# A gate's early load behind a numbered piece, and rings of four places in the first half of an output projection

## The chip, the cores and the metric

The kernel runs on one core of a Trainium2 chip. The metric is device time in microseconds from the runs' own clock. A core has TensorE (PE in the profile, its weight loads PEld), VectorE (DVE), ScalarE (ACT), GpSimd (POOL) and SyncE (SP). SyncE does no arithmetic here: it issues nearly all transfers, in order, and waits where one of them must wait.

## The reference

One layer: a norm, a modulation from the conditioning vector c, a gated short convolution between two projections, a gated residual and a last norm. All in float32, for 256 tokens, width D = 2048, inner width E = 4096.

```python
h = rmsnorm(x, norm_g)
mod = silu(c) @ ada_w + ada_b
shift, scale, gate = split(mod, 3)
h = h * (1 + scale) + shift
b_gate, c_gate, v, g = split(h @ w_in, 4)          # w_in: 2048 x 16384
u = causal_depthwise_conv(c_gate * v, conv_w)      # 3 taps
y = (b_gate * u * silu(g)) @ w_out                 # w_out: 4096 x 2048
return rmsnorm(x + gate * y, final_g)
```

## The kernel before

Each factor of a product is split in a high and a low part, rounded to TensorE's one-pass float32 form: `hi` by a cast on ScalarE (L380), `lo` by a subtraction on VectorE (L385). A product is three matmuls: high by high, low by high, high by low. The tokens h lie transposed in SBUF in both parts (`hT`, 16 groups k of 128 rows); the weights come in *pieces* of 1 MB, loaded by SyncE into rings of buffers, split, and multiplied.

The stages, with the names that the profile's lines bear:

- Start: x, its norm, the first sums of the modulation.
- `mm_s` (L545): half of the columns of w_in, while the modulation's shift and scale are still being summed.
- `mm_b` (L545), the *two-tile stage*: the other half, in 64 pieces (8 pairs of column tiles x 4 quarters x 2 halves of k). A piece is one load (L804), one high and one low part, and 48 products (2 tiles x 8 k x 3).
- The output projection, first for columns 0 to 1023 (`mm_w`, banks `mm_1`, `mm_7`), then for 1024 to 2047 (`mm_o`), L888. A piece covers two k of w_out by 1024 columns. A *plain* piece takes 24 matmuls. The pieces 8 to 15 (in the second half 10 to 15) use seven block products in place of eight (`seven`, 21 matmuls): they need sums of the weights' blocks (`sums_o`, three operations on VectorE, L769 to L773) and `forms` of the tokens' blocks.
- The end: residual, last norm, stores.

Beside the two-tile stage two more jobs run. The gate: 32 loads of ada_w (`at_g`), multiplied and summed on VectorE (`gacc`, L709, L711), then folded over the partitions by GpSimd in seven rounds of transfer and addition (L715 to L717) and added to the row `gate_row` in DRAM (L719), once for each 512 columns. And `early_weights`, which after each of certain pieces does a unit of later work: the sums of a sevens piece for columns 1024 to 2047, or one of two pieces already multiplied by the gate (`gated`); both are stored to DRAM (`made`) and loaded in the output stage. The dictionary `EARLY` says after which piece (counted from 0) which unit comes. One unit is the gate's early load (L786): 512 columns of `gate_row`, broadcast over the partitions into `turned`, a part of the scratch tile z, for the gated pieces.

What sets the order: within `short_conv_layer` a scheduler places each engine's instructions by priority, a timeline that it models, and the dependences it is given; `tc.add_manual_dep` adds one that only fixes an order. A queue is then served in that order: an instruction that waits holds up all behind it on its engine. L786 had no tie of that kind.

Places: the pool `wpool` has three buffers each of the kinds raw, hi and lo. In the output stage pieces and sums go to the lo buffers and low parts to the raw buffers. The large tile `big` takes the room of `hT` once the tokens are read; it holds x, the weights of the last norm (`fg`) and a scratch tile, and before that three more places for pieces and sums in the first 1024 columns (`wide_ring`, a ring of six) and one in the second (`next_ring`).

Of the kernel before, what the change touches and what calls it, by code (L numbers as in the profile page):

```python
# [117 lines left out]
def short_conv_layer(ctx: ExitStack, tc: tile.TileContext, x, c, norm_g, ada_w, ada_b, w_in, conv_w, w_out, final_g, out):  # L118
# [19 lines left out]
        return slots.tile(shape, dtype, tag="slot", name=name)  # L138

    nth = {"raw": 0, "hi": 0, "lo": 0}  # L140

    def pad(n, name, pool=wpool):
        pool.tile([P, n], F32, tag=name, name=name, bufs=1)

    def w_tile(kind, name, dtype=F32, i=None):

        if i is None:
            i = nth[kind] % 3
            nth[kind] += 1
        return wpool.tile([P, SLOT], dtype, tag=f"{kind}{i}", name=name, bufs=1)  # L150

    pad(32, "line4")
# [146 lines left out]
    junk = hpool.tile([P, TT, HX], F32, tag="big", name="junk")  # L299
    for t in range(TT):  # L300
        for dh in range(2):
            if t == 0:
# [12 lines left out]

    KB = KT - 2
    hT = hpool.tile([P, KB, 2 * T], F32R, tag="big", name="hT")
    hT2 = hpool.tile([P, KT - KB, 2 * T], F32R, tag="big2", name="hT2")  # L320

    def tokens(k, part):
        return (hT[:, k] if k < KB else hT2[:, k - KB])[:, part * T : (part + 1) * T]

    hh_ = [tokens(k, 0) for k in range(KT)]
    hl_ = [tokens(k, 1) for k in range(KT)]
# [347 lines left out]
    nc.gpsimd.dma_start(gate_row, ada_b[0:1, 2 * D : 3 * D])  # L674

    def gate_columns(c0, n):
        flat = gate_slots[c0 // 1024].rearrange("p h s f -> p (h s f)").bitcast(F32)
# [5 lines left out]
    def load_gate(j):  # L683

        c0 = j * 1024
        nc.sync.dma_start(gate_columns(c0, 1024), gate_row[0:1, c0 : c0 + 1024].partition_broadcast(P))

    gate_todo = [(dc, j) for dc in range(4) for j in range(0, KT, 2)]
    gacc = [None]
# [75 lines left out]
    passed = [0]  # L765

    def sums_of(b, s):

# [6 lines left out]
    def early_weights():  # L775

        while to_store:
            unit, sums = to_store.pop()
            made[unit] = dram.tile([P, SLOT], F32, tag=f"made{len(made)}", name="made")
            nc.scalar.dma_start(made[unit], sums)  # L780
        unit = EARLY.get(passed[0])
        passed[0] += 1
        if unit is None:
            return
        if unit == "gate":
            nc.sync.dma_start(turned, gate_row[0:1, 3 * W : 4 * W].partition_broadcast(P))  # L786
            return
        raw, sums = raw_tile("raw_u"), w_tile("lo", "sums_u")
        blocks, out = (v.rearrange("p (b f) -> p b f", f=W) for v in (raw, sums))
        if not isinstance(unit, int):  # L790
            load_o(raw, unit[1] * EP, EP, 3 * W, W)
            nc.vector.tensor_tensor(out=out, in0=blocks, in1=turned.unsqueeze(1).to_broadcast([P, EP, W]), op=ALU.mult)
        else:
            load_o(raw, 2 * unit, 2, 2 * W, 2 * W)
            list(sums_of(blocks, out))
        to_store.append((unit, sums))

    for ct in range(NS, NCT, 2):
        for q in QUARTERS:
            bank = psum.tile([P, CT, T], F32, tag="mm", name="mm_b")[:, 0:2]  # L800
            col = q * E + ct * P
            for kp in range(0, KT, KP):
                raw = raw_tile("raw")
                nc.sync.dma_start(  # L804
                    raw.rearrange("p (k f) -> p k f", k=KP),
                    w_in[0, kp * P : (kp + KP) * P, col : col + 2 * P].rearrange("(k p) f -> p k f", p=P),
                )
                hi, lo = split(raw, SLOT)
                for m in range(2):
                    for i in range(KP):  # L810
                        k = kp + i
                        o = slice((i * 2 + m) * P, (i * 2 + m + 1) * P)
                        for j in range(3):
                            product(bank[:, m, :], hi[:, o], lo[:, o], k, j, k == 0 and j == 0, m == 0, k == KT - 1 and j == 2)
                gate_piece()
                early_weights()
            z = zs[q // 2][:, q % 2]
            if q == 1:
                nc.scalar.copy(z, bank)
                zc = z  # L820
            elif q == 2:
                nc.vector.tensor_tensor(out=zc, in0=bank, in1=zc, op=ALU.mult)
                for j in range(2):
                    conv(ct + j, z[:, j, :], zc[:, j, :])
                u = z
            elif q == 3:
                ended_silu[0] = nc.scalar.activation(z, bank, AF.Silu)
                nc.vector.tensor_tensor(out=u, in0=u, in1=z, op=ALU.mult)
            else:
                nc.vector.tensor_tensor(out=u, in0=bank, in1=u, op=ALU.mult)  # L830
                split_y(ys[ct // 2], u)
                if ct // 2 in SEVEN:
                    token_forms(ct // 2, u)
# [2 lines left out]
        gate_piece()  # L836


    big = hpool.tile([P, 3 * D + W], F32, tag="big", name="big")
    xh = big[:, 0 : TT * D].rearrange("p (h t f) -> p h t f", h=2, t=TT)  # L840
    HD = D // 2

    def xr(t, c0, n):
        return xh[:, c0 // HD, t, c0 % HD : c0 % HD + n]

    def load_x(h):
        for t in range(TT):
            nc.sync.dma_start(xh[:, h, t], x[t * P : (t + 1) * P, h * HD : (h + 1) * HD])

    fg = big[:, TT * D : 3 * D]  # L850
    u2 = big[:, 3 * D :]
    ends = [z.rearrange("p a b f -> p (a b f)").rearrange("p (h f) -> p h f", h=2) for z in zs]

    places6 = [None] * 3 + [big[:, i * SLOT : (i + 1) * SLOT] for i in range(3)]
    taken, ending = [0], [False]

    def wide_ring(name):

        i = taken[0] % 6 if not ending[0] else 0
        taken[0] += 1  # L860
        return w_tile("lo", name) if places6[i] is None else places6[i]
# [35 lines left out]
    def weighted(t, c0, n, pr, at):  # L897


        r = xr(t, c0, n)  # L900
        nc.scalar.activation(pr, r, AF.Square, scale=D**-0.5, accum_out=fsq[:, t, at : at + 1])
        nc.vector.tensor_tensor(out=r, in0=r, in1=fg[:, c0 : c0 + n], op=ALU.mult)

    def seven(j, raw, sums, ready, bank, p1, p6, p75, opens, last):

# [34 lines left out]
        add(ends[0][:, 0], p75[:, 1], u2)  # L940
        add(ends[1][:, 0], p75[:, 1], ends[1][:, 1])

    def columns(c0, order, sevens, bank, p1, p6, p75, whole, loads=None, ring=None):


        for n, j in enumerate(order):
            raw = w_tile("raw", "raw_o") if n == 0 and c0 == 0 else ring("raw_o")
# [8 lines left out]
            if loads:  # L956
                loads(n)
            if j in sevens:
                sums = ring("sums_o")
                if ready:  # L960
                    nc.sync.dma_start(sums, made[j])
                seven(j, raw, sums, ready, bank, p1, p6, p75, j == sevens[0], j == sevens[-1])
                if j == sevens[-1]:
                    gather(p1, p6, p75)
                continue
            hi, lo = split(raw, SLOT, "raw")
# [13 lines left out]
    def wide_bank(name):  # L980
# [3 lines left out]
    wide = [wide_bank("mm_w") for _ in range(TT)]  # L984
    columns(
        0, (0, 1, 8, 2, 9, 3, 10, 4, 11, 5, 12, 13, 6, 14, 15, 7), SEVEN,
        lambda t, d: wide[t][:, d], *extra_banks(), p75, True, load_ends, wide_ring,
    )
    for t in range(TT):
        c = ends[t].rearrange("p h f -> p (h f)")  # L990
# [7 lines left out]
    def finish(t):  # L998
# [4 lines left out]
        for c0, n, vector in ((0, 512, True), (512, 512, False), (1536, 512, True), (1024, 512, False)):  # L1003
            dd = slice(c0, c0 + n)
            r = xr(t, c0, n)
            if c0 == 1536:
                nc.vector.scalar_tensor_tensor(out=r, in0=po[t], scalar=fs, in1=fg[:, dd], op0=ALU.mult, op1=ALU.mult)
# [7 lines left out]
    taken[0] = 0  # L1015

    def next_ring(name):

        i = taken[0] % 4
        taken[0] += 1  # L1020
        return big[:, SLOT : 2 * SLOT] if i == 3 and taken[0] <= 12 else w_tile("lo", name)

    halves = [wide_bank("mm_o") for _ in range(2)]
    p75 = wide_bank("mm_7")
    po = extra_banks()
    columns(
        2 * W, (0, 1, 10, 2, 11, 3, 12, 13, 8, 14, 15, 9), SEVEN_2,
        lambda t, d: halves[d][:, t], *po, p75, False, lambda n: load_x(1) if n == AT_X else None, next_ring,
    )

    def out_mm(bank, t, ep, hi, lo):
# [78 lines left out]
```

## Time and profile before

| | |
|---|---|
| runs | 919.80, 920.08, 920.12 us; median 920.08 |
| the profiled execution | 917.02 us, span 915.2 us |
| mean granted TensorE clock | 0.991 |
| read from HBM, written | 237.86 MB, 10.50 MB |
| DMA over the span | 281 GB/s mean |
| TensorE on the chain that ended last | 79% (mm_s 38%, mm_b 27%) |

The profile is of one execution, and that one was 3 us shorter than the median; durations are read from it, differences are then set against the median. A busy share of an engine is over the whole span. The chain of work is followed back from the last instruction: what released each step, or the instruction before it on its engine. In rows of single instructions the bracket holds the idle time ahead of it and what ended it.

### The profile page before, as it was taken

To read this page: it belongs to the slowest core of one execution; us is meant where nothing else is said; L and a number is where in the kernel's file an instruction comes from. 1 tells how busy PE (TensorE), PEld (TensorE's weight loads), DVE (VectorE), ACT (ScalarE), POOL (GpSimd) and SP (SyncE) were. 2 spreads that over 40 slices of the span, in tenths; PEclk is the share of its full clock that TensorE was granted. 3 is DMA by queue.
4 is the path that set the end of the run, shared out by engine and by line. 5 is a ranking of instruction groups with operands and counts; after the bars stand their busy time and mean duration, and the time that the engine had idled before them with its cause. 6 is when DMAs were issued, how large, how long until landed. Compare 5 with 4: busy or idle time off the path is not lost.

```text
span 915.2 us, 16520 instructions
## 1 busy us (share of the span) xinstructions
PE 888.6 (97%) x6977; PEld 849.9 (93%) x6977; DVE 695.4 (76%) x693; ACT 490.5 (54%) x436; POOL 88.0 (10%) x108
## 2 busy tenths in 40 slices
PE   7999999999999999999999999949999999999996
PEld 4999999999999999999999999949999988778885
DVE  5889998889987876858865786537667668999775
ACT  6768866565558765644344434234434454545553
POOL 0000000010000234410132012400000000000000
PEclk9999999999999999999999999979999999999999
DMA  9999999999997688777877889489889877686872
GB/s 307 368 370 365 365 321 354 341 363 351 380 344 258 189 279 238 237 215 222 271 230 219 273 270 307 142 286 301 290 286 289 306 264 244 197 294 235 302 280 92
DMA packets 164873, 257.29 MB, mean 281 GB/s; under 512 B 7668, under 2 KB 106580, under 8 KB 162624
## 3 DMA queue, kind: packets, MB, share of 16 engines
q1 hardware_dynamic: 159680, 239.89, 79.5%
q0 software_dynamic: 3840, 7.94, 3.2%
q10 hardware_dynamic: 1280, 8.43, 2.3%
q8 instruction: 54, 0.88, 0.4%
q14 instruction: 19, 0.16, 0.0%
HBM read 237.86 MB, written 10.50 MB: 271 GB/s over the span
## 4 chain that ended last, share of the span: by engine, by line
PE 79%; DMA 11%; DVE 4%; ACT 2%; POOL 2%; issue 1%; SPq 0%; ACTq 0%; POOLq 0%; DVEq 0%
PE mm_s L545 38%; PE mm_b L545 27%; PE mm_o L888 6%; PE mm L888 4%; DMA z<-gacc 3%; PE mm_w L888 3%; DMA at_g<-in_ada_w_dram 3%; DVE lo L385 2%; DMA at<-in_ada_w_dram 2%; ACT hi L380 2%; POOL gacc L717 1%; DMA raw_o<-in_sc_w_out_dram 1%; DMA raw<-in_sc_w_in_dram 1%; POOL z L715 0%; DVE gacc L711 0%
## 5 line engine op out<-in xcount | busy, mean ns | idle before, releaser
L545 PE MATMUL mm_b<-hT,hi 128*128 128x256 f32 x2048 | 349.9, 277 | 11.4 <-ACT hi L380 11.4
L545 PE MATMUL mm_s<-hT,hi 128*128 128x256 f32 x2048 | 336.3, 277 | 0.0
L545 PEld LDWEIGHTS mm_b<-hT,hi 128*128 128x128 f32 x2048 | 309.3, 188 | 11.6 <-ACT hi L380 11.6
L545 PEld LDWEIGHTS mm_s<-hT,hi 128*128 128x128 f32 x2048 | 299.7, 188 | 0.2
L545 PE MATMUL mm_b<-hT,lo 128*128 128x256 f32 x1024 | 283.4, 277 | 1.5 <-DVE lo L385 1.5
L545 PE MATMUL mm_s<-hT,lo 128*128 128x256 f32 x1024 | 261.7, 277 | 0.0
L380 ACT CAST hi<-raw 128x2048 fp32r<-128x2048 f32 (+1 forms) x66 | 123.8, 1876 | 206.9 <-PE mm_b L545 94.0
L385 DVE TENSOR_TENSOR lo<-raw,hi 128x2048 fp32r<-128x2048 f32 (+1 forms) x66 | 153.3, 2328 | 78.6 <-ACT hi L380 63.1
L545 PEld LDWEIGHTS mm_b<-hT,lo 128*128 128x128 f32 x1024 | 192.9, 188 | 1.8 <-DVE lo L385 1.8
L545 PEld LDWEIGHTS mm_s<-hT,lo 128*128 128x128 f32 x1024 | 182.7, 188 | 0.0
L385 DVE TENSOR_TENSOR lo<-raw_s,hi 128x2048 fp32r<-128x2048 f32 (+1 forms) x80 | 149.0, 1868 | 29.9 <-ACT hi L380 29.3
L380 ACT CAST hi<-raw_s 128x2048 fp32r<-128x2048 f32 (+2 forms) x81 | 124.0, 1541 | 70.2 <-PE mm_s L545 42.9
L515 DVE SCALAR_TENSOR_TENSOR gv<-at,silu_c,gv 128x512 f32<-128x512 f32 x105 | 78.8, 751 | 10.3 <-DMA at<-in_ada_w_dram 8.6
L568 ACT COPY acc<-mm_s 128x1024 f32<-128x1024 f32 x54 | 54.6, 1011 | 26.9 <-PE mm_s L545 26.8
L717 POOL TENSOR_TENSOR gacc<-gacc,z 128x512 f32<-128x512 f32 x28 | 44.2, 1577 | 103.4 <-DMA z<-gacc 103.4
L888 PE MATMUL mm_w<-hi,y 128*128 128x512 f32 x160 | 51.4, 390 | 0.3 <-ACT hi L380 0.3
L711 DVE SCALAR_TENSOR_TENSOR gacc<-at_g,silu_c,gacc 128x512 f32<-128x512 f32 x60 | 45.0, 749 | 7.4 <-DMA at_g<-in_ada_w_dram 6.3
L888 PE MATMUL mm_o<-hi,y 128*128 128x512 f32 x152 | 48.3, 389 | 0.0
L582 ACT COPY mm_s<-acc 128x1024 f32<-128x1024 f32 x38 | 38.6, 1015 | 2.6 <-DVE acc L571 1.8
L380 ACT CAST hi<-raw_o 128x2048 fp32r<-128x2048 f32 x14 | 26.7, 1909 | 22.1 <-DMA raw_o<-in_sc_w_out_dram 16.8
L385 DVE TENSOR_TENSOR lo<-raw_o,hi 128x2048 fp32r<-128x2048 f32 x14 | 32.1, 2289 | 6.8 <-ACT hi L380 6.7
L888 PEld LDWEIGHTS mm_w<-hi,y 128*128 128x128 f32 x160 | 30.0, 188 | 6.9 <-ACT hi L380 0.7
(191 smaller groups left out, 745.6 us busy)
## 6 DMA issues: line engine op xcount, KB each, us to landing
raw<-in_sc_w_in_dram SPq DMA_DIRECT2D x64, 1024.0 KB, 6.2
raw_s<-in_sc_w_in_dram SPq DMA_DIRECT2D x47, 1024.0 KB, 8.2
at<-in_ada_w_dram SPq DMA_DIRECT2D x126, 256.0 KB, 7.9
raw_o<-in_sc_w_out_dram SPq DMA_DIRECT2D x17, 1024.0 KB, 6.0
raw_s<-in_sc_w_in_dram SPq DMA_DIRECT2D x33, 512.0 KB, 7.2
at_g<-in_ada_w_dram SPq DMA_DIRECT2D x32, 512.0 KB, 8.2
raw_u<-in_sc_w_out_dram SPq DMA_DIRECT2D x8, 1024.0 KB, 5.7
made<-sums_u ACTq DMA_DIRECT2D x8, 1024.0 KB, 6.9
```

The lines of the kernel that those rows point to most:

```text
L380: nc.scalar.copy(hi[:, :n], raw[:, :n])
L385: last_low[0] = nc.vector.tensor_tensor(out=lo[:, :n], in0=raw[:, :n], in1=hi[:, :n].bitcast(F32), op=ALU.subtract)
L515: nc.vector.scalar_tensor_tensor(out=gv, in0=at4[:, i], scalar=c_k, in1=gv, op0=ALU.mult, op1=ALU.add)
L545: mm = last_mm[0] = nc.tensor.matmul(dst, w, h[k], start=begins and left, stop=ends, skip_group_check=True)
L568: nc.scalar.copy(acc[ch, q], bank)
L582: nc.scalar.copy(bank, acc[ch, q])
L711: nc.vector.scalar_tensor_tensor(out=ga, in0=at3[:, i, :], scalar=s, in1=ga, op0=ALU.mult, op1=ALU.add)
L717: nc.gpsimd.tensor_tensor(out=ga, in0=ga, in1=turned, op=ALU.add)
L888: nc.tensor.matmul(dst, y[a], b, start=opens and i == 0, stop=ends and i == 2, skip_group_check=True)
```

## The change

Two parts, and moves that come with them.

The gate's early load gets a dependence on the load of the 56th piece of the two-tile stage, so it stands behind it on SyncE. The sums move from pieces 35, 39, ... 55 to 32, 36, ... 52, the gate's load from 58 to 55, the gated pieces from 59 and 62 to 56 and 60.

`hT` becomes five tiles (`b0`, `b1`, `b2` of four k each, `b3` and `big2` of two), each given back when its own readers are done; `junk` and later x (`xr`), the last norm's weights and gate (`closing`) and the scratch `u2` take their places one by one. In the first 1024 output columns b0, b1 and b2 serve as a fourth buffer for pieces and sums (lo), for high parts (hi) and for low parts (raw), until the eleventh piece (n = 10); from the fourteenth (n = 13) b1 is the fourth lo buffer, until the sixth piece of the second half. The rings of six and four are gone. The gate's columns 0 to 1023 are loaded into the second half of `closing`, 1024 to 2047 into the place of piece 8's forms; the last norm's weights are loaded in two halves. `opens` and `last` of the sevens pieces now go by the order of the pieces.

```diff
     nth = {"raw": 0, "hi": 0, "lo": 0}
+    fourth = {}
...
         if i is None:
-            i = nth[kind] % 3
-            nth[kind] += 1
+            size = 4 if kind in fourth else 3
+            i = nth[kind] % size
+            nth[kind] = i + 1
+        if i == 3:
+            return hpool.tile([P, SLOT + 64], dtype, tag=fourth[kind], name=name)[:, 16 : 16 + SLOT]
         return wpool.tile([P, SLOT], dtype, tag=f"{kind}{i}", name=name, bufs=1)
...
-    hT = hpool.tile([P, KB, 2 * T], F32R, tag="big", name="hT")
-    hT2 = hpool.tile([P, KT - KB, 2 * T], F32R, tag="big2", name="hT2")
+    hT = [hpool.tile([P, SLOT + 64], F32R, tag=f"b{g}", name="hT") for g in range(3)]
+    hT += [hpool.tile([P, 4 * T], F32R, tag=tag, name="hT") for tag in ("b3", "big2")]
...
-    EARLY = {35 + 4 * i: j for i, j in enumerate(SEVEN_2)}
-    EARLY.update({58: "gate", 59: ("gated", LAST[0]), 62: ("gated", LAST[1])})
+    EARLY = {32 + 4 * i: j for i, j in enumerate(range(10, 16))}
+    EARLY.update({55: "gate", 56: ("gated", LAST[0]), 60: ("gated", LAST[1])})
...
         if unit == "gate":
-            nc.sync.dma_start(turned, gate_row[0:1, 3 * W : 4 * W].partition_broadcast(P))
+            load = nc.sync.dma_start(turned, gate_row[0:1, 3 * W : 4 * W].partition_broadcast(P))
+            tc.add_manual_dep(load.ins, last_load[0].ins.name, after, reason="the gate is done by then")
             return
...
     def load_ends(n):
 
-        ending[0] = n >= AT_END
-        if n == AT_END - 2:
-            load_gate(0)
+        if n == AT_END - 3:
+            fourth.clear()
         elif n == AT_END:
             load_x(0)
-        elif n == AT_END + 1:
-            nc.sync.dma_start(fg, final_g.rearrange("(o d) -> o d", o=1).partition_broadcast(P))
-            load_gate(1)
-
+            closing.append(hpool.tile([P, D], F32, tag="b2", name="closing"))
+            load_fg(0)
+            load_broadcast(HD, gate_row[0:1, 0:HD])
+            fourth["lo"] = "b1"
+
+    fourth.update({"lo": "b0", "hi": "b1", "raw": "b2"})
...
+    def load_last(n):
+
+        if n == AT_X - 3:
+            fourth.clear()
+        elif n == AT_X:
+            load_x(1)
+            nc.sync.dma_start(gate_columns(HD, HD), gate_row[0:1, HD:D].partition_broadcast(P))
+            load_fg(1)
```

How it moves SyncE's queue in the second half of the two-tile stage (raw: pieces, raw_u: the early units' weights, z: the gate's early load). Before:

```order
L804 DMA raw<-in_sc_w_in_dram 128x8x256 x4
L755 DMA raw_u<-in_sc_w_out_dram 128x2x1024
L804 DMA raw<-in_sc_w_in_dram 128x8x256 x4
L755 DMA raw_u<-in_sc_w_out_dram 128x2x1024
L786 DMA z_4482<-gate_row 128x512
L804 DMA raw<-in_sc_w_in_dram 128x8x256 x4
```

The same queue after, from the fifth early unit:

```order
L757 DMA raw_u<-in_sc_w_out_dram 128x2x1024
L808 DMA raw<-in_sc_w_in_dram 128x8x256 x4
L757 DMA raw_u<-in_sc_w_out_dram 128x2x1024
L808 DMA raw<-in_sc_w_in_dram 128x8x256 x3
L789 DMA z_4485<-gate_row 128x512
L808 DMA raw<-in_sc_w_in_dram 128x8x256
L757 DMA raw_u<-in_sc_w_out_dram 128x4x512
```

The gate's load stood behind the 40th piece and the second early unit; it now stands behind the 56th and the sixth.

TensorE where the two-tile stage ends and the output begins (mm_w and mm_1 are banks; hi_8428 and lo_8430 are the parts of piece 0, hi_8458 of piece 1, hi_8489 of piece 8, the third in turn). Before:

```order
L545 MATMUL mm_b_8291<-hT2_174,lo_8354 128x256
L888 MATMUL mm_w_8422<-hi_8428,y0_3413 128x512
L888 MATMUL mm_w_8422<-lo_8430,y0_3413 128x512
L888 MATMUL mm_w_8422<-hi_8428,y0_3413 128x512 x2
L888 MATMUL mm_w_8422<-lo_8430,y0_3413 128x512
```

After (hi_8431 and lo_8433 are the parts of piece 0, hi_8492 of piece 8):

```order
L550 MATMUL mm_b_8300<-hT_177,lo_8359 128x256
L891 MATMUL mm_w_8425<-hi_8431,y0_3416 128x512
L891 MATMUL mm_w_8426<-hi_8431,y0_3416 128x512
L891 MATMUL mm_1_8427<-hi_8492,y8_4475 128x512
L891 MATMUL mm_w_8425<-lo_8433,y0_3416 128x512
```

The first matmul of piece 8 stood behind all of piece 0 and two matmuls of piece 1; it now stands third, ahead of the first use of piece 0's low part.

SyncE in the output's first half. Before, from the sixth piece on (big: places of the ring of six, x and the last norm's weights; gate: the gate's halves):

```order
L755 DMA raw_o<-in_sc_w_out_dram 128x2x1024 x2
L686 DMA gate_4480<-gate_row 128x1024
L755 DMA big<-in_sc_w_out_dram 128x2x1024 x2
L686 DMA gate_4481<-gate_row 128x1024
L755 DMA raw_o<-in_sc_w_out_dram 128x2x1024 x2
L755 DMA big<-in_sc_w_out_dram 128x2x1024 x2
L755 DMA raw_o<-in_sc_w_out_dram 128x2x1024 x2
L848 DMA big<-in_x_dram 128x1024 x2
L961 DMA big<-made 128x2048
L871 DMA big<-in_final_g_dram 128x2048
```

After, from the stage's start:

```order
L757 DMA raw_o<-in_sc_w_out_dram 128x2x1024 x7
L1024 DMA gate_4483<-gate_row 128x1024
L757 DMA raw_o<-in_sc_w_out_dram 128x2x1024 x5
L852 DMA xr<-in_x_dram 128x1024 x2
L858 DMA closing<-in_final_g_dram 128x1024
L858 DMA closing<-gate_row 128x1024
L757 DMA raw_o<-in_sc_w_out_dram 128x2x1024 x6
```

One of the two loads of the gate behind which pieces stood is gone from there; x, half of the last norm's weights and half of the gate stand in front of the 13th piece, where x and the weights stood behind the 15th.

More of the change, by code (lines that the diff above doesn't have):

```diff
@@ L298, in short_conv_layer @@
     rstd = const.tile([P, TT], F32, tag="rstd", name="rstd")
-    junk = hpool.tile([P, TT, HX], F32, tag="big", name="junk")
+    junk = hpool.tile([P, TT, HX], F32, tag="b0", name="junk")
     for t in range(TT):
@@ L941, in gather, with columns @@
         add(ends[1][:, 0], p75[:, 1], ends[1][:, 1])
-    def columns(c0, order, sevens, bank, p1, p6, p75, whole, loads=None, ring=None):
+    def columns(c0, order, sevens, bank, p1, p6, p75, whole, loads=None):
+        in_turn = [j for j in order if j in sevens]
         for n, j in enumerate(order):
-            raw = w_tile("raw", "raw_o") if n == 0 and c0 == 0 else ring("raw_o")
+            raw = w_tile("raw" if n == 0 and c0 == 0 else "lo", "raw_o")
             ready = c0 > 0 and j in made
@@ L958, in columns @@
             if j in sevens:
-                sums = ring("sums_o")
+                sums = w_tile("lo", "sums_o")
                 if ready:
                     nc.sync.dma_start(sums, made[j])
-                seven(j, raw, sums, ready, bank, p1, p6, p75, j == sevens[0], j == sevens[-1])
-                if j == sevens[-1]:
+                seven(j, raw, sums, ready, bank, p1, p6, p75, j == in_turn[0], j == in_turn[-1])
+                if j == in_turn[-1]:
                     gather(p1, p6, p75)
```

50 lines of the change are left out of this document (22 added, 28 removed).

## The prediction

> **What bounds the kernel now.** I read the page first: busy shares, then the slices (two of its 40-slice lines, TensorE's busy tenths and granted clock).
>
> ```profile
> PE 888.6 (97%) x6977; PEld 849.9 (93%) x6977; DVE 695.4 (76%) x693; ACT 490.5 (54%) x436; POOL 88.0 (10%) x108
> PE   7999999999999999999999999949999999999996
> PEclk9999999999999999999999999979999999999999
> ```
>
> TensorE is the bound, at 97% of 915.2 us. It has one hole in mid-kernel: in the 27th slice (595 to 618 us) it is busy four tenths, and its clock falls. The waits of TensorE (waited for: total us, times, longest) say how much all its holes are worth:
>
> ```profile
> PE mm_b L545 <- ACT hi L380: 11.4, 1, 11.4
> PE mm_b L545 <- DVE lo L385: 1.5, 1, 1.5
> PE mm L888 <- DVE lo L918: 1.0, 2, 0.6
> PE mm_w L888 <- ACT hi L380: 0.3, 1, 0.3
> ```
>
> The first two are the hole; the last two, 1.3 us, are all else that an edit after the start can win. The chain of work that ended last names the cause (start, length, what):
>
> ```profile
> 377.06 125.02 PE mm_b L545 x1103
> ...
> 542.97 0.55 POOL z L715
> ...
> 593.92 2.13 DMA gate_row<-gacc
> 596.25 0.34 SPq L786
> 596.70 7.37 DMA raw<-in_sc_w_in_dram
> 604.15 1.91 ACT hi L380
> 606.08 2.30 DVE lo L385
> 608.42 126.55 PE mm_b L545 x1102
> ```
>
> The gate row's last transfer ends at 596.05. SyncE's L786 (the gate's early load) goes 0.2 us later, the next piece behind it, and that piece's landing, high part and low part precede TensorE's restart. SyncE's own waits confirm it: it stood at L786 for 15.9 and 3.8 us.
>
> ```profile
> SPq L786 <- DMA z<-gacc: 15.9, 1, 15.9
> SPq L786 <- DMA gate_row<-gacc: 3.8, 1, 3.8
> ```
>
> **The change part by part.**
>
> *The gate's load behind the 56th piece.* A piece is 48 products. At 125.02 / 1103 = 0.1133 us each it takes 5.44 us, and the stage's 64 pieces take 3072 x 125.02 / 1103 = 348.2 us. Begun at 377.06 without a hole the stage ends at 725.3. It really ended where the first product of the output starts:
>
> ```profile
> 740.23 0.39 PE L888 MATMUL mm_w<-hi,y 128*128 128x512 f32 x1
> ```
>
> So the hole costs 740.2 - 725.3 = 15.0 us. That is the idle 12.9 of the first two waits plus about 2 of slow clock, which the stretches show (length, busy and count, granted clock, DMA share, GB/s):
>
> ```profile
> 598.00:605.00 7.00, 0.00 (x0) 0.50 0.99 309
> 610.00:612.00 2.00, 2.00 (x14) 0.69 0.91 284
> 612.00:614.00 2.00, 2.00 (x20) 1.00 0.97 262
> ```
>
> After the change the load stands behind piece 56 (counted from 1). Loads run ahead: the 33rd piece was issued at 533.46 (row below) and multiplied from 377.06 + 32 x 5.44 = 551.1, 17.7 us later. The 57th would be issued near 377.06 + 56 x 5.44 - 17.7 = 664, 68 us after the row was done. Its reader, the first gated piece, moves with it. What was queued behind it on SyncE no longer waits. Saved: 15.0.
>
> *The early sums three pieces sooner.* Six sums and two gated pieces keep their count and durations; each moves three or two pieces forward. The delicate one is the first: it enters where VectorE still works off the gate's sums. SyncE's issues, VectorE's low parts, and the two landings (issue, size, us) that begin at 544.9 and at 547.5:
>
> ```profile
> 533.46 14.01 SPq L804 DMA_DIRECT2D raw<-in_sc_w_in_dram  x4
> 542.58 4.49 DVE L385 TENSOR_TENSOR lo<-raw,hi 128x2048 fp32r<-128x2048 f32 x2
> 544.90 2.57 SPq L804 DMA_DIRECT2D raw<-in_sc_w_in_dram  x2
> raw<-in_sc_w_in_dram SPq DMA_DIRECT2D x1, 1024.0 KB, 6.2
> raw<-in_sc_w_in_dram SPq DMA_DIRECT2D x1, 1024.0 KB, 9.1
> ```
>
> The low part of piece 32 ends at 544.8, 0.9 us before its need at 377.06 + 31 x 5.44 = 545.7. The added load takes a ring place, so piece 34 is loaded when that low part frees one, at 544.9. It lands 6.2 us later (551.1) if like the load issued there before, 9.1 (554.0) if like the one issued at 547.5. With 1.9 for the high and 2.3 for the low part (durations in the chain above) it is ready at 555.3 or 558.2; TensorE wants it at 556.6. So 0 to 1.6 us; I take 0, because the 6.2 is the landing of a load issued at that very moment. Could it gain? No: TensorE had no wait there.
>
> *The output's first half: rings of 4, 4 and 4 in place of 6 (pieces and sums), 3 and 3.* No arithmetic changes. Before, the shortage was of high and low parts: ScalarE's cast waits for TensorE to give back one of three places, and VectorE waits behind it. One plain piece and one sevens piece on VectorE, then ScalarE:
>
> ```profile
> 764.21 2.29 DVE L385 TENSOR_TENSOR lo<-raw_o,hi 128x2048 fp32r<-128x2048 f32 x1 [0.96 <-ACT hi L380]
> 766.42 1.22 DVE L769 TENSOR_TENSOR sums_o<-raw_o 128x1024 f32<-128x1024 f32 x1
> 769.01 1.75 DVE L918 TENSOR_TENSOR lo<-raw_o,hi 128x1536 fp32r<-128x1536 f32 x1
> 771.14 2.29 DVE L385 TENSOR_TENSOR lo<-sums_o,hi 128x2048 fp32r<-128x2048 f32 x1 [0.38 <-ACT hi L380]
> 774.41 2.29 DVE L385 TENSOR_TENSOR lo<-big,hi 128x2048 fp32r<-128x2048 f32 x1 [0.97 <-ACT hi L380]
> 772.47 1.91 ACT L380 CAST hi<-big 128x2048 fp32r<-128x2048 f32 x1 [1.36 <-PE mm_w L888]
> ```
>
> ```profile
> 824.00:880.00 56.00, 56.00 (x248) 46.25 (x247) 43.64 (x26) 31.20 (x22) 0.00 (x0) 1.00 0.81 278
> ```
>
> The last row is TensorE's output without a hole: 56.00 / 248 = 0.226 us a matmul. The pair's period is 774.41 - 764.21 = 10.20, of which VectorE waits 0.97 + 0.38; its own work is 8.85. With a fourth place it gains 1.35 us a pair on TensorE, over seven pairs, until the ring is full. That lead pays for the two places where sevens pieces are neighbours (12, 13 and 14, 15), where VectorE needs 2 x (8.85 - 2.25) = 13.2 us against TensorE's 2 x 21 matmuls, 9.5, and where the 1.3 us of waits lie. Against it the fourth places go at the eleventh piece, and 2 MB (x, weights, gate) now stand on SyncE in front of the 13th piece instead of 15 pieces down; at the 309 GB/s above they are 6.5 us, within the 9.5 of the two sevens pieces ahead. I take 0.9 of the 1.3 as won; the ends are 1.3 won and, if the lead isn't built, 1.3 lost again.
>
> *The output's start.* TensorE's order moves here (shown with the change). A matmul of piece 8 now stands third in the stage, where before it stood behind all of piece 0; so TensorE needs that piece at once. And the low part of piece 0 now lies in the place that the third group of tokens leaves, whose last reader stands 12 products before the two-tile stage's end. VectorE may write it from 12 x 0.113 = 1.4 us before that end and needs 2.3: ready 0.9 us after it, wanted after three matmuls, 0.7. I count 0.5 lost, with a handover of a few tenths. Piece 8's load waits only for a low part whose readers end two pieces (10.9 us) before the stage does; 6.2 of landing and 1.9 of cast fit in that, 9.1 and 1.9 are late by 0.1. Range 0.2 to 3, the far end for a landing of some 12. SyncE's wait for TensorE behind the seventh piece stays (the gate's other half goes where piece 8's forms lie, free 69 matmuls or 15.6 us into the stage); the piece queued behind it is wanted only after 159 matmuls, 36 us, so it costs nothing.
>
> *The output's second half.* The second half of x (1 MB) is issued some 20 us sooner, and 0.5 MB of the last norm's weights moves over from the first half. The old stretch, the row of 824 to 880, had no hole, so nothing can be gained; its transfers came to 278 GB/s and the slots of TensorE's hole moved 309 with room, so I take 0, and 1.5 as the far end for one piece that lands late.
>
> Sum: -15.0 + 0 + 0.5 - 0.9 + 0 = -15.4. The profiled execution took 917.0 us (span 915.2), the median of the runs 920.08; the same 15.4 off gives 901.6 and **904.7**.
>
> **The rivals.**
>
> *Part of the hole comes back* (a late first sum 1.6, the start 3, the second half 1.5, the 1.3 lost again): 2 to 7 us, 907 to 912. For it speaks that every slack above is about 1 us; against it that TensorE had no other wait over 0.6. A pause might also cost clock: the rows show it halved in a pause of 12.9 us, at some 2 us, and full in pauses of 0.6. [...]
>
> *The change doesn't do what it says*: the gate is late for piece 56 as well. It would need a delay of 68 us in a chain on GpSimd that took 53 (542.97 to 596.05 in the chain above); then little is won, 918 to 920.
>
> *Slower: the ring of four starves VectorE.* It holds pieces and sums together, three places a pair. The plain piece after next may be loaded only when this pair's sums are split, so two periods are at least landing + cast + 8.85. At landing 6.2 a period is (6.2 + 1.9 + 8.85) / 2 = 8.5, at 9.1 it is 9.9, both under TensorE's 10.20. To eat 15.4 us over seven periods it must reach 12.4, a landing of 14. One load here took that, with the hole's four issued together:
>
> ```profile
> raw<-in_sc_w_in_dram SPq DMA_DIRECT2D x1, 1024.0 KB, 14.5
> ```
>
> All of them so slow gives 920 to 922. The median landing of these loads is under half of it, so I give it little:
>
> ```profile
> raw_o<-in_sc_w_out_dram SPq DMA_DIRECT2D x17, 1024.0 KB, 6.0
> ```
>
> **How the numbers follow.** Forecast (903 to 907) 0.72; part of the hole back 0.21; no effect 0.03; slower 0.04. The three runs lie within 0.3 us; 0.2% (1.8 us) is about what can be told from no change. The low end is every wait gone: 15.0 + 1.3 and 0.8 for the runs' spread and for terms rounded up, 903.0. The high end takes in most of the returning hole, 910. Faster 0.94, same 0.03, slower 0.03.
>
> **What would show it.** Right: SyncE's wait at the gate's early load gone, the clock at full from start to end, mm_b lasting 348 us, and TensorE's waits under 2 us after the start. The first sum: a wait of mm_b near 556 or none. The start: a wait of mm_w for VectorE's lo of 0.2 to 1. The rings: VectorE's gaps of 0.97 gone, waits of mm for lo at pieces 12 to 15 gone. Wrong would be mm_b at 350 or more, products slower than 0.1133 us from tokens in four tiles at new places (each 1 ns is 6 us over 6144 products), or waits of the output for loads.

## The result, and the profile after

The changed kernel took 905.98 us (median of 5 runs, 904.27 to 906.42), beside 919.80 us for the kernel before on the same chip (5 runs, 915.45 to 920.12). The ratio is 0.9857, with a 95% interval of 0.9835 to 0.9879. The prediction was 904.7 us, range 903 to 910: the direction and the size came out, but one term of the sum failed, and that the time came so near is partly luck (see below). Two runs of the experiments, one of them of the kernel before, were disturbed (915.33 and 1504.39 us, at a lower clock) and are left out of medians, ranges and ratios.

The profiled execution took 905.98 us with a span of 904.2 us. Its page, the busy shares and the two slice lines of TensorE:

```profile
PE 886.3 (98%) x6977; PEld 846.8 (94%) x6977; DVE 695.1 (77%) x693; ACT 491.6 (54%) x436; POOL 93.7 (10%) x108
PE   7999999999999999999999999999999999999986
PEclk9999999999999999999999999999999999999999
```

The hole of the 27th slice is gone, and the granted clock is 0.9 or more in every slice. In the chain of work mm_b is one row (start, length, what):

```profile
376.11 346.95 PE mm_b L550 x3060
```

No wait of mm_b is left, and mm_b runs through in one piece. SyncE's wait at the gate's early load is gone too. But TensorE now waits 5.2 us in the output, where before it waited 1.3. Its timeline puts each wait in its place (start, duration, then in the bracket the idle time ahead and what ended it):

```profile
725.43 0.50 PE L891 MATMUL mm_w<-lo,y 128*128 128x512 f32 x1 [0.32 <-DVE lo L390]
808.89 0.50 PE L891 MATMUL mm<-hi,y 128*128 128x512 f32 x1 [1.56 <-ACT hi L920]
848.61 0.50 PE L891 MATMUL mm<-lo,form 128*128 128x512 f32 x1 [0.53 <-DVE lo L390]
864.39 0.51 PE L891 MATMUL mm<-lo,form_h 128*128 128x512 f32 x1 [0.33 <-DVE lo L390]
867.62 0.73 PE L891 MATMUL mm_o<-hi,y 128*128 128x512 f32 x2 [0.88 <-ACT hi L385]
869.95 0.50 PE L891 MATMUL mm_o<-lo,y 128*128 128x512 f32 x1 [1.59 <-DVE lo L390]
```

One wait stands at the start, one at the switch from the first half of the output columns to the second, and four at 845 to 870 us. Set side by side, each stage from its first matmul to the next stage's first (the last to the end of the last matmul), in us of the profiled executions:

| | two-tile stage | output, first half | output, second half |
|---|---|---|---|
| before | 363.3 | 84.5 | 83.2 |
| after | 348.3 | 84.6 | 88.1 |

So the two-tile stage gave 15.0, and the second half took 4.9 back. Two things must be kept in mind with this table. The idle time ahead of a stage's first matmul counts to the stage before, so the 1.56 us at the switch stand in the first half's 84.6, not in the 4.9. And a wait costs more than its bracket says: matmuls of the output start 0.23 us apart (the last ten in plain float32 of the same size, `tp_idle` at the kernel's start, 0.44), and around that wait they start 1.95 and 0.34 us apart (at 806.94, 808.89 and 809.23 us), which is 1.8 us lost for a bracket of 1.56.

### The profile page after: what moved, and what is told of

Read it like the earlier page. It is cut to its first block, busy times and chain, and to the rows that moved or that the text cites. A ratio compares the mean times of both kernels' runs of the same rounds, so it can differ in the third digit from the quotient of the medians.

```text
span 904.2 us, 16521 instructions
## 1 busy us (share of the span) xinstructions
PE 886.3 (98%) x6977; PEld 846.8 (94%) x6977; DVE 695.1 (77%) x693; ACT 491.6 (54%) x436; POOL 93.7 (10%) x108
## 4 chain that ended last, share of the span: by engine, by line
PE 89%; DMA 5%; DVE 3%; ACT 2%; issue 1%; SPq 0%; ACTq 0%
PE mm_s L550 39%; PE mm_b L550 38%; PE mm_w L891 6%; PE mm L891 3%; PE mm_o L891 3%; DMA at<-in_ada_w_dram 2%; DVE lo L390 2%; DMA raw_o<-in_sc_w_out_dram 2%; DMA sums_o<-made 1%; ACT hi L385 1%; DVE lo L921 1%; ACT hi L920 0%; DVE sums_o L772 0%; PE sum L423 0%; SPq L244 0%
## 5 line engine op out<-in xcount | busy, mean ns | idle before, releaser
L550 PE MATMUL mm_b<-hT,hi 128*128 128x256 f32 x2048 | 348.3, 276 | 0.0
L390 DVE TENSOR_TENSOR lo<-raw,hi 128x2048 fp32r<-128x2048 f32 (+1 forms) x66 | 150.7, 2286 | 60.4 <-ACT hi L385 57.4
L390 DVE TENSOR_TENSOR lo<-raw_o,hi 128x2048 fp32r<-128x2048 f32 x18 | 41.0, 2288 | 17.9 <-ACT hi L385 11.4
L385 ACT CAST hi<-raw_o 128x2048 fp32r<-128x2048 f32 x18 | 34.4, 1909 | 26.5 <-DMA raw_o<-in_sc_w_out_dram 16.2
L390 DVE TENSOR_TENSOR lo<-sums_o,hi 128x2048 fp32r<-128x2048 f32 x14 | 32.1, 2292 | 11.5 <-ACT hi L385 11.4
```

Of the source, the lines that this page charges most:

```text
L385: nc.scalar.copy(hi[:, :n], raw[:, :n])
L390: last_low[0] = nc.vector.tensor_tensor(out=lo[:, :n], in0=raw[:, :n], in1=hi[:, :n].bitcast(F32), op=ALU.subtract)
L550: mm = last_mm[0] = nc.tensor.matmul(dst, w, h[k], start=begins and left, stop=ends, skip_group_check=True)
```

## The experiments

Each was timed in 5 or more runs beside the kernel before on its own chip. The medians of the kernel before lay between 916.8 and 919.8 us on these chips, so across chips the ratios count first. Stage lengths are worked out as in the table above, from one profile of each kernel.

**The tie alone** (the kernel before, its rings and its places kept; the lines that keep each piece's load in `last_load` are left out here):

```diff
-            nc.sync.dma_start(turned, gate_row[0:1, 3 * W : 4 * W].partition_broadcast(P))
+            load = nc.sync.dma_start(turned, gate_row[0:1, 3 * W : 4 * W].partition_broadcast(P))
+            tc.add_manual_dep(load.ins, last_load[0].ins.name, after, reason="the gate is done by then")
```

> The kernel before with the tie alone (its rings 6/3/3, its places 58/59/62 and its second half kept). Theory A: the pause was the wait of the gate's load at SyncE, ahead of the loads of the last pieces, and the tie alone takes away all 15 us of it; it also keeps before's second half of the output, which after ran 4.9 us slower. So 901 to 905 us, no wait of mm_b over 0.5 us, and an output stage of about 168 us. Theory B: the tie needs the sums of the early weights to be moved too, or the fourth buffers; then at least 5 us of the pause stay, 909 us or more, with a wait of mm_b in the trace.

Measured: 901.41 us (901.12 to 901.69), ratio 0.9831 [0.9812, 0.9851]. Groups of TensorE by line, and its waits in that stage and after it:

```profile
L545 PE MATMUL mm_b<-hT,hi 128*128 128x256 f32 x2048 | 348.2, 276 | 0.0
```

```profile
PE mm L890 <- DVE lo L920: 1.0, 2, 0.6
PE mm_w L890 <- ACT hi L380: 0.5, 1, 0.5
```

mm_b takes 348.2 us and waits for nothing. The two halves take 84.8 and 83.5 us, within 0.3 us of before. Theory A: the tie is the whole gain. The rest of the change costs time: on the same chip two kernels with the whole change and one small edit each took 905.2 us (the first of x's later loads and the first of the ties at the switch, below).

**The change without the tie** (the added dependency left out, all else kept):

> The changed kernel without the tie alone (rings 4/4/4 and the new places kept). Theory A: SyncE waits at the gate's load again and mm_b pauses for 12 to 15 us: 917 to 921 us. Theory B: rings and places carry part of the gain: 907 to 914 us, with a pause of under 8 us.

Measured: 919.01 us (916.73 to 921.17), ratio 1.0023 [1.0007, 1.0038]. SyncE's waits and TensorE's stretches (length, busy and count, granted clock, DMA share, GB/s):

```profile
SPq L789 <- DMA z<-gacc: 12.4, 1, 12.4
SPq L789 <- DMA gate_row<-gacc: 3.7, 1, 3.7
```

```profile
600.00:605.00 5.00, 0.00 (x0) 0.75 0.99 297
605.00:610.00 5.00, 0.79 (x2) 0.50 1.09 346
```

The wait at SyncE, the pause and the fall of the clock are all back, though TensorE's pause is shorter than Theory A named (9.7 us in two waits; the stage lasts 361.7). Rings and places carry none of the gain.

**No tie, but the gate's load on GpSimd's queue:**

```diff
-            load = nc.sync.dma_start(turned, gate_row[0:1, 3 * W : 4 * W].partition_broadcast(P))
+            load = nc.gpsimd.dma_start(turned, gate_row[0:1, 3 * W : 4 * W].partition_broadcast(P))
```

> The changed kernel without the tie, and with the gate's early load issued by GpSimd instead of SyncE. Theory A: the pause is SyncE's queue standing behind that one wait, not the gate's lateness; with the load on a queue that holds no pieces there is no pause of mm_b even without the tie: 904 to 906.5 us. Theory I: it is the late gate itself (VectorE's product of gate and weights, or the rings held by it), so that mm_b pauses again for 8 us or more: 914 to 921 us.

Measured: 907.38 us (904.89 to 909.58), ratio 0.9886 [0.9859, 0.9913]. This time lies 0.9 us above Theory A's range, and far below Theory I's. GpSimd issues the load as soon as the row is whole; SyncE issues pieces before that moment and after it:

```profile
607.75 0.59 POOL L789 DMA_DIRECT2D z<-gate_row  x1 [5.18 <-DMA gate_row<-gacc]
```

```profile
589.02 11.47 SPq L807 DMA_DIRECT2D raw<-in_sc_w_in_dram  x4
609.44 12.34 SPq L807 DMA_DIRECT2D raw<-in_sc_w_in_dram  x4
```

The row is even later than before, 607.7 us, and there is no pause at it (mm_b's one wait in this profile is 1.7 us, at 564). So it was not the gate's lateness, but the queue that stood behind the wait. The tie and another queue do the same; the 1.4 us over the changed kernel's median lie within the runs' spread.

**The tie with the new places** (the kernel before; the early sums at 32 to 52, the gate and the gated pieces at 55, 56 and 60):

> The kernel before with the tie and with the new places of the early sums and gated pieces (32 to 52, 55, 56 and 60), its rings and second half kept. Theory A: the places cost and bring nothing: as with the tie alone, 900.8 to 902 us. Theory B: they move loads into the stretch where all transfers are busiest (0.9 to 1.0 of the DMA engines from 550 to 610 us), and mm_b waits there: 902.5 us or more, with waits of mm_b of 1 us or more.

Measured: 902.58 us (901.11 to 904.00), ratio 0.9834 [0.9809, 0.9858], against 901.41 with the tie alone, on another chip. Its stretches:

```profile
560.00:570.00 10.00, 9.76 (x86) 1.00 0.97 293
600.00:610.00 10.00, 8.64 (x76) 1.00 0.92 294
```

mm_b waits 1.6 us in two places where the DMA engines are over 0.9 busy. The time is at the edge of Theory B's range, and by the ratios the two theories can't be told apart. The stage lengths point to Theory B, taken over all profiles with a tie or with the load moved: with the new places the two-tile stage took 348.2 to 351.1 us (ten kernels, mean 349.6; two of them 348.2), with the old places 348.2 both times (the tie alone, and the last kernel below). The cast and VectorE ahead of the first of these waits (at 561.65 us) show more than busy transfers:

```profile
554.32 1.92 ACT L380 CAST hi<-raw 128x2048 fp32r<-128x2048 f32 x1 [1.98 <-DMA raw<-in_sc_w_in_dram]
556.79 0.69 DVE L481 TENSOR_TENSOR y<-z,y 128x512 fp32r<-128x512 f32 x1 [1.72 <-ACT y L480]
558.70 0.69 DVE L752 TENSOR_TENSOR form<-z,form 128x512 fp32r<-128x512 f32 x1 [0.69 <-ACT form L751]
559.31 2.29 DVE L385 TENSOR_TENSOR lo<-raw,hi 128x2048 fp32r<-128x2048 f32 x1
```

The high part was done at 556.24, and the low part began 3.1 us later: in VectorE's order the last steps of y and of a form of the tokens stand in front of it, and there VectorE waits 1.72 and 0.69 us for ScalarE. The same order stands in front of the second wait. With the tie alone, at the old places, the low part of that time stands ahead of y.

**Rings of three in the first half** (`fourth.update(...)` left out):

> The changed kernel without the fourth buffers for pieces, high and low part in the first 1024 output columns (three of each throughout). Theory J: with three low places loads are issued late, as in the second half, where some seven pieces on three places cost 3.3 us; over 13 pieces that is 4 to 6 us: 910 to 912 us, with waits of mm_w in the trace. Theory K: VectorE's 8.85 us a pair against TensorE's 10.2 leave room enough, and three do: 905.5 to 907 us.

Measured: 906.28 us (905.56 to 908.07), ratio 0.9882 [0.9861, 0.9903]: Theory K by the time. The trace shows that the fourth places do something: the first half takes 86.8 us in place of 84.6, with these two waits that the changed kernel has not.

```profile
754.18 0.51 PE L890 MATMUL mm<-hi,y 128*128 128x512 f32 x1 [0.86 <-ACT hi L916]
801.84 0.50 PE L890 MATMUL mm<-lo,y 128*128 128x512 f32 x1 [0.78 <-DVE lo L920]
```

Its second half waited less in that execution (85.4 us against 88.1). Some 2 us that the fourth places win in front were not there at the end.

**x's second half asked for later** (AT_X 10, then 11, in place of 8). The number also says how long the low part keeps its fourth place, since x takes that place over: up to the sixth piece with 8, the eighth with 10, the ninth with 11 (the second expectation counts one too few).

> The changed kernel with x's second half asked for two pieces later in the second half of the output (its number AT_X 10 instead of 8), which also keeps the low part's fourth place two pieces longer. Theory C: the 3.3 us that TensorE waits from 845 to 870 us of the changed kernel come from x's early 1 MB and the ring's return to three; then they fall to 0.5 us or less, and the time by 2.5 to 3.3, to 902.7 to 903.5 us. Theory D: they come from the loads of the pieces themselves, which land late whatever stands beside them: 905.5 to 906.5 us, with waits of 3 us at the same pieces. The 1.6 us at the start of the second half stay under both.

> The changed kernel with x's second half asked for three pieces later (AT_X 11 instead of 8), so that the low part's fourth place lasts to the eighth piece of the second half, about as long as before's (12 tiles). Theory C, in its stronger form: the casts wait on loads as soon as the ring is back to three; kept so long, the waits of TensorE from 845 to 870 us fall from 3.3 us to 0.5 or less, and the time to 902.7 to 903.5 us. Theory D: 905 to 906.5 us, with waits of 1.5 us or more there.

Measured: with 10, 905.15 us (904.06 to 905.89), ratio 0.9870 [0.9850, 0.9890]; with 11, 903.37 us (902.51 to 904.70), ratio 0.9852 [0.9829, 0.9875]. What ScalarE's casts waited for from 808 to 875 us, in the changed kernel and then with 11:

```profile
ACT hi L385 <- DMA sums_o<-made: 8.1, 4, 2.7
ACT hi L385 <- DMA raw_o<-in_sc_w_out_dram: 6.2, 4, 3.7
ACT hi L920 <- DMA raw_o<-in_sc_w_out_dram: 3.4, 3, 1.9
```

```profile
ACT hi L385 <- DMA raw_o<-in_sc_w_out_dram: 3.0, 2, 2.1
ACT hi L385 <- DMA sums_o<-made: 2.9, 2, 1.6
ACT hi L920 <- DMA raw_o<-in_sc_w_out_dram: 1.5, 1, 1.5
```

17.7 us of waiting for loads became 7.4, and the second half fell from 88.1 over 86.2 (with 10) to 83.9 us, with no wait of TensorE after the switch. With 10, 1.8 of the 3.3 us stayed, and the time is just under Theory D's range. With 11 the trace and the time are Theory C's, but the ratio can't be told from the changed kernel's 0.9857. The number moves two things, the transfer of x and the ring's width. Here is the first cast of the stage that waits for a piece's load; of the changed kernel, of 10 and of 11 (timelines of ScalarE, and of SyncE for x in the last):

```profile
833.78 1.48 ACT L920 CAST hi<-raw_o 128x1536 fp32r<-128x1536 f32 x1 [1.35 <-DMA raw_o<-in_sc_w_out_dram]
```

```profile
849.05 1.91 ACT L385 CAST hi<-raw_o 128x2048 fp32r<-128x2048 f32 x1 [2.74 <-DMA raw_o<-in_sc_w_out_dram]
```

```profile
851.49 1.48 ACT L920 CAST hi<-raw_o 128x1536 fp32r<-128x1536 f32 x1 [1.54 <-DMA raw_o<-in_sc_w_out_dram]
852.30 0.81 SPq L852 DMA_DIRECT2D xr<-in_x_dram  x2
```

They are the pieces 12, 8 and 14, in each kernel the first that is loaded into the ring of three. With 11 the wait comes before x is issued at all, so it needs no traffic of x. In the other two x goes out 1.7 and 2.9 us ahead of that piece's load, and the two causes aren't told apart.

Nor is the ring the whole of it. Of the changed kernel's 3.3 us, 2.8 stand at the last three pieces (864 to 870 us), which are loaded into a ring of three in all these kernels. Their loads (count, size, median us from issue to landing), of the changed kernel, of the first tie at the switch (the next run) and with 11:

```profile
raw_o<-in_sc_w_out_dram SPq DMA_DIRECT2D x3, 1024.0 KB, 7.6
raw_o<-in_sc_w_out_dram SPq DMA_DIRECT2D x3, 1024.0 KB, 5.2
raw_o<-in_sc_w_out_dram SPq DMA_DIRECT2D x3, 1024.0 KB, 5.6
```

The run with the tie has the changed kernel's rings and asks for x at the same piece, and TensorE waited only 0.2 us after the switch. So with the same ring of three TensorE waited 2.8 us at landings of 7.6 us and hardly at 5.2: here the time of landing decided whether it waited. Why the loads landed later in one profile than in the other isn't shown, and Theory D is not excluded. Over all profiles, TensorE's waits after the switch, those at 824 to 827 us in the runs below left out, are 0.2 to 3.3 us with 8 (six kernels), 1.8 with 10 and 0 to 0.8 with 11 (four kernels).

**The switch of the halves.** First piece 10's first matmul was tied behind piece 0; then also VectorE's low part of piece 1 behind the gathering of the first half's sums (the lines that set `first_piece` and `gathered` are left out):

```diff
+            if opens and i == 0 and first_piece[0]:
+                tc.add_manual_dep(mm.ins, first_piece[0].ins.name, after, reason="the first piece comes first")
```

```diff
+            if n == 1 and c0:
+                tc.add_manual_dep(last_low[0].ins, gathered[0].ins.name, after, reason="the banks come free first")
```

> The changed kernel with one more tie: in the second half of the output the first matmul of piece 10 stands behind all of piece 0's. Theory E: it stood first there, and the 1.6 us for which TensorE waited for its high part go: 904.2 to 904.6 us, with no wait of over 0.3 us at 807 us. Theory F: the high part was late for its own reasons, and the wait shows again some matmuls on, or is made good by the waits at 845 to 870 us, which shrink when TensorE comes later: 905.7 to 906.3 us.

> The changed kernel, with piece 10's first matmul behind piece 0 in the second half of the output (as in the run before), and VectorE's low part of piece 1 behind the gathering of the first half's last sums, whose four additions free the bank of piece 0. Theory G: the 1.5 us for which TensorE waits at 808 us are that gathering, which VectorE ended only at 808.69 us (809.68 us in the run with the one tie) because it put a low part of 2.28 us between its additions; with these together it ends 2.3 us sooner, the wait falls to 0.2 us or less, and the time by 1.3 to 1.6, to 903.6 to 904.6 us. Theory H: the cast of piece 10 holds TensorE all the same, or piece 1's low part is then late by as much: 905 to 906.5 us, with 1 us or more of waits between 805 and 815 us.

Measured: 905.18 us (903.52 to 908.42), ratio 0.9875 [0.9854, 0.9897], between Theories E and F; and 905.90 us (904.04 to 908.30), ratio 0.9877 [0.9854, 0.9901], Theory H by the time. With the first tie alone TensorE stood as long as ever, now ahead of piece 0; here are TensorE and the last of VectorE's gathering:

```profile
809.83 0.47 PE L893 MATMUL mm_o<-hi,y 128*128 128x512 f32 x1 [1.53 <-ACT hi L925]
809.00 0.68 DVE L944 TENSOR_TENSOR z<-mm,z 128x512 f32<-128x512 f32 x1
```

The bracket names piece 10's cast. The second run shows that piece 0 doesn't need it: there VectorE gathers early, and piece 0 starts on time, at 807.08, before that cast has begun.

```profile
805.87 0.68 DVE L945 TENSOR_TENSOR z<-mm,z 128x512 f32<-128x512 f32 x1
807.08 0.39 PE L894 MATMUL mm_o<-hi,y 128*128 128x512 f32 x1
807.28 1.48 ACT L926 CAST hi<-raw_o 128x1536 fp32r<-128x1536 f32 x1 [3.31 <-PE mm_w L894]
```

So two things of the same length lay on top of each other at the switch, the order of TensorE and the end of the gathering. By these traces both must go (the second tie was not run without the first). Then the first half takes 82.9 us. But the time did not move: TensorE stands again 18 us on, at piece 10's sums, whose cast comes out of a stretch in which ScalarE has no pause from 815.67 to 824.82 us, two squares of the first half's closing (at 817.48 and 818.53) in it.

```profile
824.87 0.73 PE L894 MATMUL mm<-hi,form 128*128 128x512 f32 x2 [1.31 <-ACT hi L385]
822.92 1.90 ACT L385 CAST hi<-sums_o 128x2048 fp32r<-128x2048 f32 x1
```

**Three combinations.** Both ties with AT_X 11; the same with the closing of the first half put off on VectorE; and AT_X 11 with the old places:

> The changed kernel with the two ties of the gathering (as in the run of 905.9 us) and x's second half asked for at the eleventh place (as in the run of 903.37 us). Theory M: the 1.5 us at 808 us and the 3 us at 845 to 870 us are two separate losses, and both go: 901.5 to 902.3 us. Theory N: VectorE has no pause from 797 to 828 us, since the closing of the first half (some 9.5 us of sums and products) stands between the low parts there; TensorE, 1.5 us earlier, waits 1.3 us at 825 us as in the run of 905.9 us: 902.8 to 903.8 us.

> The kernel with both (ties of the gathering, x's second half at the eleventh place), and VectorE's last four operations of the first half's closing put off: the two additions to x behind the low part of piece 10's sums, the two products with the final norm behind that of piece 11's sums. Theory N: the wait at 825 us goes then, 901.3 to 902.3 us, with waits of TensorE in the second half of the output under 0.5 us together. Theory P: the low parts that come after the four operations are late instead, or the loads are: 902.8 us or more.

> The changed kernel with x's second half asked for at the eleventh place (the run of 903.37 us) and with the old places of the early sums and gated pieces (35 to 55, 58, 59 and 62) kept. Theory Q: the account closes, three terms side by side: the second half's narrow ring (2.6 us, already gone), the new places (1.2 us, 902.58 against 901.41) and the 1.56 us at the switch of the halves less what the four places save in the first half (some 1 us). So 901.7 to 902.7 us, no wait of mm_b over 0.3 us. Theory R: the places cost nothing, and 902.58 us was chance: 903 to 904 us, with waits of mm_b as before.

Measured: 903.65 us (901.76 to 906.38), ratio 0.9848 [0.9823, 0.9873]; 905.48 us (903.30 to 906.00), ratio 0.9863 [0.9839, 0.9886]; 903.94 us (901.89 to 905.97), ratio 0.9856 [0.9830, 0.9882]. The first has the wait of 1.31 us again, at 826.20 (Theory N's time; ScalarE is as full there as VectorE, with no pause from 816.99 to 826.15 us). The second has 0.86 there, for a low part, and Theory P's time:

```profile
826.43 0.50 PE L895 MATMUL mm_o<-lo,y 128*128 128x512 f32 x1 [0.86 <-DVE lo L390]
```

The third has no wait of mm_b, as Theory Q wanted, and a median that is Theory R's; it still waits 1.56 us at the switch and 0.52 at 851 us. These last three can't be told from each other. None beats the tie alone.

## Why the prediction was right, and where it was not

*The gate's load (15.0).* Right: the stage lasts 348.2 us with the tie alone, 361.7 without the tie, and has no hole with the load on another queue. The load went out at 657.15 us, where 664 was forecast, 52 us after the row was done in that execution (604.90). The worked sum, one stage's products times their duration against the stage's real end, gave the gain to a tenth.

*The early sums (0, range 0 to 1.6).* Mis-sized. The profiled execution of the changed kernel shows nothing, but in ten profiles with the new places the stage was 1.4 us longer in the mean, at most 2.9. The waits come one piece later than forecast, at 561 to 564 us, and again at 600 to 607, which the sum did not look at. In the profile with the tie and the new places the forecast's piece landed in 6.6 us and was in time; the next one landed in 8.3 and was not. But the landing was not the whole step: the sum let a low part begin as soon as the high part was done, and VectorE had y and a form in front of this one. In the changed kernel VectorE has the same order, and there it was just in time.

*The first half's rings (0.9 won of 1.3).* Right in the way, under-sized. The brackets fell from 1.3 us to 0 to 0.7 in the profiles with four places, the start apart (0.4 was forecast), and stand at 1.9 with three everywhere. In length it is some 2.2 us: 84.5 before against 82.9 with both ties, which have 0.6 of the start's loss in them, and 86.8 against 84.6 with rings of three. A bracket is less than a wait costs. The sign named for it was wrong: VectorE's gaps are still there (1.21, 0.94 and 1.59 us in the changed kernel), ended by ScalarE's casts.

*The start (0.5 lost).* Right: a bracket of 0.32 us (0.6 from start to start), for the cause forecast, piece 0's low part; 0.56 in the last kernel.

*The second half (0, far end 1.5).* This step failed: it lost 4.9, and 1.7 more at the switch in front of it. Three things were missed. The argument went by transfers, with room in GB/s, and left out when loads may be issued: the low part's fourth place goes three pieces before x is asked for, so the ring is back to three from the seventh piece. The far end allowed for one piece that lands late; the last three took 7.1 to 7.8 us. How the loss divides between the two stays open. And the price of a new order was worked out for the start of the first half, but not for the start of the second, where the same kind of matmul moved to the front; it was one of two things that held TensorE there for 1.56. By the prediction's own signs this part was wrong: waits under 2 us after the start were to show it right (their brackets come to 4.9), and waits of the output for loads were to show it wrong.

The time came out nearer than the terms, and that is partly luck. Between the profiled executions the difference is 11.0 us (917.02 to 905.98): 15.0, 2.2 of the rings and 1.0 by which the stages ahead were shorter, less 0.6 at the start, 1.7 at the switch and 4.9. Between the medians of that chip it is 13.8, since before's profiled execution lay 3 us under its median, and there 15.4 was forecast. The prediction took the runs to lie within 0.3 us; before's five runs lie 4.7 apart.

The rival "part of the hole comes back" (907 to 912) had the second half among its places, but with 1.5 us, and the hole did not come back. It counted its pauses at their length alone: a single one of 2.16 us kept the clock at 1.00, four short ones close together did not (last section). Starvation of the ring of four, the slower rival, is excluded: TensorE's waits in the first half, the start and the switch apart, are no longer than 0.15 us.

What stays open is why the tie alone is so steady (0.6 us between its runs) and all others with a tie vary by 2 to 5, even the one that has only the new places beside it.

## What to carry to other kernels

A load that waited for a late producer held all that stood behind it on SyncE's queue (12.4 and 3.7 us without the tie, and 9.7 us of TensorE's time; no pause at it with the load on GpSimd's queue): tie such a load behind what it need not pass, or give it a queue where nothing urgent stands. Test each part of a change alone: here one line was the gain, 901.4 us, and the rest of the edit cost more than it brought. And when a buffer is handed from a ring to a later use, count which piece first meets the narrow ring, and ask whether it stands the slowest landing on record, not the usual one; the room between 278 and 309 GB/s, on which the forecast counted, did not keep the second half from losing 4.9 us.

## What the runs showed of the hardware that was not expected

Several short waits close together were followed by a fall of the clock, without any long one. With the gate's load on GpSimd's queue TensorE waited 0.83, 0.20, 0.74 and 0.35 us between 851.1 and 856.8 us, and then ran at half clock for some 3 us:

```profile
851.89 0.50 PE L890 MATMUL mm<-lo,form 128*128 128x512 f32 x1 [0.83 <-DVE lo L390]
854.42 0.73 PE L890 MATMUL mm_o<-hi,y 128*128 128x512 f32 x2 [0.20 <-ACT hi L385]
855.90 0.49 PE L890 MATMUL mm<-hi,y 128*128 128x512 f32 x1 [0.74 <-ACT hi L919]
856.75 0.59 PE L890 MATMUL mm_o<-lo,y 128*128 128x512 f32 x1 [0.35 <-DVE lo L390]
```

```profile
854.00:856.00 2.00, 1.05 (x4) 1.00 0.89 360
856.00:858.00 2.00, 1.65 (x5) 0.75 0.15 51
858.00:860.00 2.00, 2.00 (x6) 0.50 0.92 256
```

The changed kernel waited 0.88 and 1.59 us between 866.7 and 870 us and kept its clock:

```profile
867.00:869.00 2.00, 0.73 (x2) 1.00 0.94 347
869.00:871.00 2.00, 1.05 (x5) 1.00 0.35 76
```

A single wait of 2.16 us, in the run with both ties, left it at 1.00 as well. So the clock fell after short waits in the first of these traces and not in the second, and no run here tells what decides. In the other profiles the short waits of the output left the clock at 1.00 (windows of 5 us from 720 to 890 us; of the last kernel the record has the mean alone, 0.998). A wait with no other near it cost some 0.3 us more than its bracket: by the starts of the matmuls, 1.8 us for 1.56 at the switch and 2.4 for 2.16 in the run with both ties.
